# Expert feed-forward of a two-layer encoder: the first pair's rows are half gathered by products, half by an indirect DMA

## The chip, the cores and the metric

The kernel runs on one core of one Trainium2 chip. The metric is device time in microseconds (us) of one execution, as the median of several runs. A lower number is better.

## What is computed

The program is two layers of an encoder over 512 tokens of width 1024. Each layer is a mixer (three kinds of attention heads) and then a feed-forward part with 16 experts, of which each chooses its own 64 tokens:

```python
def expert_choice_ffn(h, w_router, w_gate, w_up, w_down):
    cap = CAPACITY_FACTOR * S // N_EXPERTS              # 64
    logits = einsum('bsd,de->bse', h, w_router)
    affinity = softmax(logits, axis=-1)
    gate, idx = top_k(swapaxes(affinity, 1, 2), cap)    # per expert: 64 tokens
    xe = vmap(lambda hb, ib: hb[ib])(h, idx)            # the chosen rows of h
    a = einsum('becd,edf->becf', xe, w_gate)            # 1024 x 1408 per expert
    u = einsum('becd,edf->becf', xe, w_up)              # 1024 x 1408
    y = einsum('becf,efd->becd', silu(a) * u, w_down)   # 1408 x 1024
    y = y * gate[..., None]
    return scatter-add of y to the rows idx of a zero (S, D)
```

Here h is the normalised residual stream. All is float32. The change touches how the line `xe = ...` is done for the first two experts of a layer.

## The kernel before, in words

**The experts' loop.** The 16 experts are taken in 8 pairs, and a pair has one tile of 128 rows: 64 rows of each of its experts. Loop `for p in range(8)` (L1213) does a pair. For each pair the gate weights, then the up weights, then the down weights are streamed from HBM, in 8 loads each (L1219 and L1253 call `load`, which issues the DMA at L153 from the queue of SP). One load is 128 partitions of 2 x 1408 floats, 1,441,792 bytes: one block of 128 input features for both experts. So a pair has 24 loads, and a layer 192.

**The ring of buffers.** Loads land in 15 buffers (`SEQ`, L35) that are taken in turn; one of them, `hx`, serves once, so from then on it is 14. A load can be issued only when the product that read the buffer's previous content is done. While the attention part still runs, SP has already issued the first 15 loads of the layer (gate 0 to 7 and up 0 to 6 of pair 0). Load 15 waits for the product with load 0, load 16 for the one with load 1, and so on to load 26; from load 27 on a load waits for the product 14 loads before it. Counted so, loads 8 to 15 are pair 0's up weights, 16 to 23 its down weights, and load 24 is the first gate load of pair 1.

**Products.** For feature block k of a pair the product is L1222: 12 instructions of TensorE, with `xe[:, k]` (features on partitions, the pair's 128 rows along the free axis) as stationary operand, and the weights moving. `keep_in_program_order` pins the products to the order in which the code is written; other instructions may be moved by the scheduler.

**How a pair's rows come into `xe`.** There are two ways.

- By products, for pair 0 alone. `places(0)` (L1123) makes a 0/1 selection matrix `at` from the router's ranks, scaled by the rows' normalisation factors. `fill(at, xe, k, n, pin)` (L1136) multiplies block k of the residual stream `x`, which is in SBUF, with it (L1142) and copies the result with a gain into `xe` (L1145, VectorE). The table `EARLY` (L57) says after which gate product which block is filled: block 0 ahead of the loop, blocks 1 and 2 after product 0, and one more block after each of the products 1 to 5.
- By an indirect DMA, for pairs 1 to 7. `marks(p)` (L1147) makes the selection matrix `oh` once more (VectorE), multiplies it with a small table (L1154) to get the token number and the scale of each row, transposes it for the later scatter (L1156), and copies the numbers to SBUF (L1158 to L1162). `fetch_rows(p)` (L1166) then has GpSimd start a DMA that reads 128 rows of 4 KB from the DRAM copy `xrow_d` of the residual stream (written before, L1025), and ScalarE scales them (L1170). `turn_rows` (L1173) transposes four 128x128 pieces of the rows (L1177) and copies them with the gain into `xe` (L1178). For pair p + 1 `marks` and `fetch_rows` stand after gate product 6 of pair p, and the two calls of `turn_rows` in the code after the up product of pair p (L1242). These transposes weren't pinned.

`marks(0)` (L1229) is needed for pair 0's scatter alone; it stands after up product 2 of pair 0.

**After the up product** of a pair silu(a) * u is formed (L1237 on ScalarE, L1238 on VectorE), transposed (L1246), copied (L1247) and multiplied with the down weights (L1259). The next pair's gate products carry the scatter of this pair's result (L1198).

Of the kernel before, what the change touches and what calls it, by code (L numbers as in the profile page):

```python
# [11 lines left out]
F32 = mybir.dt.float32  # L12
F32R = mybir.dt.float32r
# [9 lines left out]
P = 128  # L23
S = 512
D = 1024
L = 2
NT = S // P
# [26 lines left out]
PLAN = [(0, 1), (1, 1), (2, 2), (3, 2), (4, 2), (0, 0), (1, 2), (5, 2)]  # L54
PART_ON = 'vvav'
START = [[6, 0, 2, 6, 4], [2, 0, 0, 4, 2]]
EARLY = [[(0, 1)], [(1, 1), (2, 1)], [(3, 1)], [(4, 1)], [(5, 1)], [(6, 1)], [(7, 1)], [], []]  # L57
END_ON = 'avavav'
MARK_AT = 6
FIRST_MARKS = 2  # L60
SCATTER_AT = (2, 4)
HALVED = 8
EASE = 5
# [66 lines left out]
def body(ctx, tc, x_in, pos, w_in, w_uq, w_ukv, w_out, w_gate, w_up, w_down, gatt, gfin, params, consts, band, sel, out):  # L130
    nc = tc.nc
# [7 lines left out]
    def nm(s):  # L139
        uid[0] += 1  # L140
        return f"{s}_{uid[0]}"

    def bank():
        return pp.tile([P, 512], F32, tag="ps", name=nm("ps"))
# [17 lines left out]
    ident = cp.tile([P, P], F32, name="ident")  # L162
# [698 lines left out]
    for l in range(L):  # L861
        with ExitStack() as es:
# [186 lines left out]
            t = NT - 1  # L1049
# [16 lines left out]
            b = bank()  # L1066
# [4 lines left out]
            b = bank()  # L1071
# [11 lines left out]
        with tc.tile_pool(name=f"fx{l}", bufs=1, reuse_waits="tile") as fx, tc.tile_pool(name=f"fw{l}", bufs=2, side="right", reuse_waits="tile") as fw:  # L1083
# [24 lines left out]
            token, scales = slots[:, 128:136].bitcast(I32), slots[:, 136:144]  # L1108
# [13 lines left out]

            def places(p):  # L1123

                at_ = fw.tile([P, D], F32, tag="xy", bufs=1, name=nm("at"))[:, :S].rearrange("p (t s) -> p t s", t=NT)
                for t in (0, 2):
                    chosen(at_, p, t, t + 2)
                for t in range(NT):
                    if t < 2:
                        nc.scalar.activation(at_[:, t], at_[:, t], AF.Copy, scale=rstds[:, t : t + 1])  # L1130
                    elif t % 2 == 0:
                        q = at_[:, t : t + 2]
                        nc.vector.tensor_tensor(q, q, rstds[:, t : t + 2].unsqueeze(2).to_broadcast([P, 2, P]), op=ALU.mult)
                return at_

            def fill(at_, xe, k0, n, pin=False):  # L1136

                b = bank()
                for k in range(n):
                    c = (k0 + k) * P  # L1140
                    for t in range(NT):
                        made = nc.tensor.matmul(b[:, k * P : (k + 1) * P], x[:, t, c : c + P], at_[:, t], start=(t == 0), stop=(t == NT - 1))  # L1142
                        if pin:
                            tc.keep_in_program_order(made)
                nc.vector.tensor_tensor(xe[:, k0 : k0 + n, :], b[:, : n * P].rearrange("p (k s) -> p k s", k=n), gf[:, k0 : k0 + n].unsqueeze(2).to_broadcast([P, n, P]), op=ALU.mult)  # L1145

            def marks(p):  # L1147

                oh = fw.tile([P, S], F32R, tag="oh", bufs=2, name=nm("oh"))
                o3 = oh.rearrange("p (t s) -> p t s", t=NT)  # L1150
                tc.keep_in_program_order(chosen(o3, p, 0, NT))
                b, g = bank(), bank()
                for t in range(NT):
                    nc.tensor.matmul(g[:, 0:4], o3[:, t].bitcast(F32), info[:, t, p, :], start=(t == 0), stop=(t == NT - 1))  # L1154
                for t in range(NT):
                    nc.tensor.transpose(b[:, t * P : (t + 1) * P], o3[:, t].bitcast(F32), ident)  # L1156
                for i in range(2):
                    nc.vector.tensor_copy(gates[64 * i : 64 * i + 64, p : p + 1], g[64 * i : 64 * i + 64, i : i + 1])  # L1158
                if p > 0:
                    nc.vector.tensor_copy(token[:, p : p + 1], g[:, 2:3])  # L1160
                    nc.vector.tensor_copy(scales[:, p : p + 1], g[:, 3:4])
                nc.vector.tensor_copy(oh, b)  # L1162
                return oh


            def fetch_rows(p):  # L1166

                v = fw.tile([P, D], F32, tag="xy", bufs=1, name=nm("rows"))
                nc.gpsimd.indirect_dma_start(v, None, xrow_d[l][:, :], bass.IndirectOffsetOnAxis(token[:, p : p + 1], 0))  # L1169
                nc.scalar.activation(v, v, AF.Copy, scale=scales[:, p : p + 1])  # L1170
                return v

            def turn_rows(v, xe, k0):  # L1173

                b = bank()
                for k in range(4):
                    nc.tensor.transpose(b[:, k * P : (k + 1) * P], v[:, (k0 + k) * P : (k0 + k + 1) * P], ident)  # L1177
                nc.vector.tensor_tensor(xe[:, k0 : k0 + 4, :], b.rearrange("p (k s) -> p k s", k=4), gf[:, k0 : k0 + 4].unsqueeze(2).to_broadcast([P, 4, P]), op=ALU.mult)  # L1178

            def gathered():  # L1180
# [27 lines left out]
            xe, xg = gathered(), places(0)  # L1208
            warm(WARM_P)
            for f in EARLY[0]:  # L1210
                fill(xg, xe, *f)
            ohs = {}
            for p in range(8):  # L1213
                acc = []
                for w in (w_gate, w_up):
                    bs = [bank() for _ in cuts]
                    acc.append(bs)
                    for k in range(KD):
                        ws = load(w[l, p, k])  # L1219
                        for b, (q0, qn) in zip(bs, cuts):  # L1220
                            for i in range(2):
                                tc.keep_in_program_order(nc.tensor.matmul(b[64 * i : 64 * i + 64, : qn * NJ], xe[:, k, 64 * i : 64 * i + 64], ws[i][:, q0 * NJ : (q0 + qn) * NJ], start=(k == 0), stop=(k == KD - 1)))  # L1222
                        if w is w_gate and p == 0:
                            for f in EARLY[k + 1]:
                                fill(xg, xe, *f, pin=True)
                        if w is w_gate and k in SCATTER_AT and pending is not None:
                            scatter(*pending, 2 * SCATTER_AT.index(k))
                        if w is w_up and k == FIRST_MARKS and p == 0:
                            ohs[0] = marks(0)  # L1229
                        if w is w_gate and k == MARK_AT and p < 7:  # L1230
                            ohs[p + 1] = marks(p + 1)
                            rows = fetch_rows(p + 1)
                hx = wide()
                hh, hT = hx[:, :FF].rearrange("p (j q) -> p j q", j=NJ), hx[:, FF:].rearrange("p (j s) -> p j s", j=NJ)
                for g, u, (q0, qn) in zip(acc[0], acc[1], cuts):
                    hv = hh[:, :, q0 : q0 + qn].rearrange("p j q -> p q j")
                    nc.scalar.activation(hv, g[:, : qn * NJ].rearrange("p (q j) -> p q j", j=NJ), AF.Silu)  # L1237
                    nc.vector.tensor_tensor(hv, u[:, : qn * NJ].rearrange("p (q j) -> p q j", j=NJ), hv, op=ALU.mult)  # L1238
                if p < 7:
                    nxt = gathered()  # L1240
                    for k0 in (0, 4):
                        turn_rows(rows, nxt, k0)  # L1242
                for j0, n in ((0, 4), (4, 4), (8, 3)):
                    b = bank()
                    for q in range(n):
                        nc.tensor.transpose(b[:, q * P : (q + 1) * P], hh[:, j0 + q, :], ident)  # L1246
                    nc.vector.tensor_copy(hT[:, j0 : j0 + n, :], b[:, : n * P].rearrange("p (q s) -> p q s", q=n))  # L1247
                bs = [bank(), bank()]
                ahead = [(t, h) for t in range(NT - 1) for h in range(2)] if p == 7 else []
                whole = {}  # L1250
                for lo in range(0, NJ * D, FF):
                    hi = lo + FF
                    ws = load(w_down[l, p, lo // FF])  # L1253
                    e = lo
                    while e < hi:
                        j, h = e // D, e % D // 512
                        z = min(hi, (e // 512 + 1) * 512)
                        for i in range(2):
                            tc.keep_in_program_order(nc.tensor.matmul(bs[h][64 * i : 64 * i + 64, e % 512 : e % 512 + z - e], hT[:, j, 64 * i : 64 * i + 64], ws[i][:, e - lo : z - lo], start=(j == 0), stop=(j == NJ - 1)))  # L1259
                        e = z  # L1260
                    if ahead and lo > 0:
                        take_x(*ahead.pop(0))
                ys = results(p, bs)
                if p < 7:
                    pending = ohs.pop(p), ys
                    xe = nxt
            yh, yl = ys
            oh = ohs.pop(7)
# [17 lines left out]
            else:  # L1286
                rows = [slot(f"s{i}") for i in range(RING)]
# [112 lines left out]
```

## Time and the profile before

| | |
|---|---|
| median of 3 runs | 1974.07 us (1973.97 to 1975.56) |
| the profiled execution's own time | 1974.58 us |
| its span, first to last instruction | 1972.8 us |
| TensorE busy (PE) | 1754.5 us, 89% of the span |
| VectorE, ScalarE, GpSimd busy | 739.9, 425.0, 290.8 us |
| HBM read | 616.55 MB |
| L1222, gate and up products | 3072 instructions, some 570 to 590 ns each |
| L1142, products that gather (both layers) | 128 instructions |
| L1177, transposes of fetched rows | 112 instructions |

An instruction's line is that of kernel.py. PE is TensorE's matmuls, DVE VectorE, ACT ScalarE, POOL GpSimd; SP issues the weight loads. "ps" is a bank of PSUM, "xslot", "slot" and "hx" are the ring's buffers, "rows" the fetched rows. Times on the axis are from the span's start. Layer 0's expert loop runs from about 351 to 984 us, that of layer 1 from about 1320 us to the end.

### The profile page before, as it was taken

To read this page: it belongs to the slowest core of one execution; us is meant where nothing else is said; L and a number is where in the kernel's file an instruction comes from. 1 tells how busy PE (TensorE), PEld (TensorE's weight loads), DVE (VectorE), ACT (ScalarE), POOL (GpSimd) and SP (SyncE) were. 2 spreads that over 40 slices of the span, in tenths; PEclk is the share of its full clock that TensorE was granted. 3 is DMA by queue.
4 is the path that set the end of the run, shared out by engine and by line. 5 is a ranking of instruction groups with operands and counts; after the bars stand their busy time and mean duration, and the time that the engine had idled before them with its cause. 6 is when DMAs were issued, how large, how long until landed. Compare 5 with 4: busy or idle time off the path is not lost.

```text
span 1972.8 us, 22329 instructions
## 1 busy us (share of the span) xinstructions
PE 1754.5 (89%) x8894; PEld 918.0 (47%) x8894; DVE 739.9 (38%) x1467; ACT 425.0 (22%) x881; POOL 290.8 (15%) x276
## 2 busy tenths in 40 slices
PE   8889999898998988888898899998998988888887
PEld 6667666433333333333386756753333433333323
DVE  7886966111111111211178778551211211211112
ACT  4226972000000000000042379411000000000001
POOL 4552431000000000000055344200000000000000
PEclk9999999999999999999999999999999999999999
DMA  6755548899999999999947546488999999999995
GB/s 220 197 164 91 121 142 322 317 402 423 424 425 424 425 424 425 424 423 425 406 128 224 141 82 158 161 334 346 425 425 424 424 425 424 425 425 424 425 424 245
DMA packets 102473, 646.72 MB, mean 328 GB/s; under 512 B 11009, under 2 KB 28161, under 8 KB 53217
## 3 DMA queue, kind: packets, MB, share of 16 engines
q1 hardware_dynamic: 88336, 606.34, 76.7%
q0 software_dynamic: 11968, 35.02, 7.6%
q10 hardware_dynamic: 2064, 3.93, 0.6%
q8 instruction: 70, 1.15, 0.2%
q14 instruction: 35, 0.28, 0.0%
HBM read 616.55 MB, written 27.39 MB: 326 GB/s over the span
## 4 chain that ended last, share of the span: by engine, by line
DMA 39%; PE 37%; DVE 14%; issue 5%; ACT 3%; POOL 1%; SPq 0%; DVEq 0%; ACTq 0%; POOLq 0%
DMA xslot<-in_w_up_dram 13%; PE ps L1222 10%; DMA xslot<-in_w_gate_dram 10%; PE ps L1259 8%; DMA xslot<-in_w_down_dram 7%; PE ps L840 4%; DMA rows<-xrow_d,slots 3%; DMA slot<-in_w_gate_dram 3%; DMA slot<-in_w_down_dram 3%; PE ps L750 2%; PE ps L741 2%; PE ps L659 2%; PE ps L642 2%; DVE sm L591 1%; DVE sw L409 1%
## 5 line engine op out<-in xcount | busy, mean ns | idle before, releaser
L1222 PE MATMUL ps<-xslot,xe 128*64 128x506 f32 (+1 forms) x2400 | 515.8, 575 | 25.5 <-DMA xslot<-in_w_up_dram 13.3
L1222 PEld LDWEIGHTS ps<-xslot,xe 128*64 128x64 f32 x2400 | 167.0, 140 | 347.3 <-issue 288.5
L1259 PE MATMUL ps<-xslot,hx 128*64 128x512 f32 (+3 forms) x1392 | 248.6, 506 | 22.3 <-DMA xslot<-in_w_down_dram 18.4
L1238 DVE TENSOR_TENSOR hx<-ps,hx 128x506 f32<-128x506 f32 (+1 forms) x48 | 42.9, 957 | 473.9 <-PE ps L1222 473.9
L1259 PEld LDWEIGHTS ps<-xslot,hx 128*64 128x64 f32 x1392 | 94.2, 137 | 164.5 <-issue 123.4
L1189 ACT ACTIVATE hx<-ps,gates 128x512 fp32r<-128x512 f32 x32 | 20.2, 683 | 674.7 <-PE ps L1259 674.7
L1169 POOL DMA_INDIRECT rows<-xrow_d,slots x14 | 13.8, 984 | 985.2 <-DVE oh L1162 913.7
L1190 DVE SCALAR_TENSOR_TENSOR hx<-ps,gates,hx 128x512 fp32r<-128x512 f32 x32 | 22.6, 747 | 344.6 <-ACT hx L1189 344.6
L1222 PE MATMUL ps<-slot,xe 128*64 128x506 f32 (+1 forms) x648 | 141.8, 573 | 7.7 <-DMA slot<-in_w_gate_dram 6.0
L741 PE MATMUL ps<-xh,w 128*128 128x512 f32 (+1 forms) x448 | 142.6, 400 | 3.1 <-DVE w L340 2.4
L1200 DVE TENSOR_TENSOR x<-ps,x 128x512 f32<-128x512 f32 x112 | 69.6, 684 | 161.9 <-PE ps L1198 161.9
L598 ACT ACTIVATE P<-ps,sm 128x512 f32<-128x512 f32 x168 | 116.4, 703 | 41.1 <-DVE sm L591 40.0
L1170 ACT ACTIVATE rows<-rows,slots 128x1024 f32<-128x1024 f32 x14 | 16.1, 1147 | 446.0 <-DMA rows<-xrow_d,slots 446.0
L328 POOL TENSOR_TENSOR slot<-slot,gcol 128x1024 f32<-128x1024 f32 (+4 forms) x46 | 88.1, 1929 | 119.8 <-PE ps L1275 109.8
L741 PEld LDWEIGHTS ps<-xh,w 128*128 128x128 f32 (+1 forms) x448 | 83.3, 187 | 25.9 <-DVE w L340 3.3
L1222 PEld LDWEIGHTS ps<-slot,xe 128*64 128x64 f32 x648 | 45.3, 139 | 93.6 <-issue 75.8
L1177 PE MATMUL ps<-ident,rows 128*128 128x128 f32 x112 | 26.7, 417 | 66.5 <-ACT rows L1170 66.5
L741 PE MATMUL ps<-xl,w 128*128 128x512 f32 (+1 forms) x224 | 85.7, 393 | 0.0
L591 DVE TENSOR_REDUCE sm<-ps 128x1 f32<-128x512 f32 x120 | 78.9, 681 | 8.1 <-PE ps L576 5.7
L642 PE MATMUL ps<-ident,P 128*128 128x128 f32 x512 | 78.0, 275 | 0.3 <-ACT P L598 0.3
L1259 PE MATMUL ps<-slot,hx 128*64 128x512 f32 (+3 forms) x400 | 71.6, 497 | 6.2 <-DMA slot<-in_w_down_dram 4.7
L750 PE MATMUL ps<-w,xh 128*128 128x320 f32 (+1 forms) x256 | 65.9, 342 | 10.4 <-DVE w L340 10.4
(280 smaller groups left out, 2299.1 us busy)
## 6 DMA issues: line engine op xcount, KB each, us to landing
xslot<-in_w_gate_dram SPq DMA_DIRECT2D x100, 1408.0 KB, 26.2
xslot<-in_w_up_dram SPq DMA_DIRECT2D x100, 1408.0 KB, 27.1
xslot<-in_w_down_dram SPq DMA_DIRECT2D x100, 1408.0 KB, 27.0
slot<-in_w_gate_dram SPq DMA_DIRECT2D x28, 1408.0 KB, 27.0
slot<-in_w_down_dram SPq DMA_DIRECT2D x28, 1408.0 KB, 27.0
slot<-in_w_up_dram SPq DMA_DIRECT2D x26, 1408.0 KB, 27.4
slot<-in_w_in_dram SPq DMA_DIRECT2D x8, 1536.0 KB, 6.8
st<-bst_d POOLq DMA_DIRECT2D x40, 256.0 KB, 4.7
```

What stands on the lines that cost most here:

```text
L328: tc.keep_in_program_order(nc.gpsimd.tensor_tensor(v, v, g, op=ALU.mult))
L591: nc.vector.tensor_reduce(mn, ps, axis=AX.X, op=ALU.min)
L598: nc.scalar.activation(e, ps, AF.Exp, bias=mn, scale=-1.0, accum_out=lcol)
L642: nc.tensor.transpose(b[:, kc * P : (kc + 1) * P], e[:, kc * P : (kc + 1) * P], ident)
L659: nc.tensor.matmul(o[64 * i : 64 * i + 64], heads[2 * m + i][4][:, kc, :], pts[i][:, kc, :], start=(kc == 0), stop=(kc == NT - 1))
L741: nc.tensor.matmul(b[:m], w[:, passes[j][0], k, :m], passes[j][1](k), start=(n == 0), stop=(n == 3 * KD - 1))
L750: nc.tensor.matmul(acc[t][:, :m], xs, w[:, c, kk, :], start=(k == 0 and j == 0), stop=(k == KD - 1 and j == 2))
L840: nc.tensor.matmul(blocks[t][1 + h], o, w[h], start=(i == 0), stop=(i == 3 * KD - 1))
L1200: nc.vector.tensor_tensor(xv, b, xv, op=ALU.add)
L1222: tc.keep_in_program_order(nc.tensor.matmul(b[64 * i : 64 * i + 64, : qn * NJ], xe[:, k, 64 * i : 64 * i + 64], ws[i][:, q0 * NJ : (q0 + q ...
L1238: nc.vector.tensor_tensor(hv, u[:, : qn * NJ].rearrange("p (q j) -> p q j", j=NJ), hv, op=ALU.mult)
L1259: tc.keep_in_program_order(nc.tensor.matmul(bs[h][64 * i : 64 * i + 64, e % 512 : e % 512 + z - e], hT[:, j, 64 * i : 64 * i + 64], ws[i][ ...
```

## The change

Pair 0 now uses both ways. Blocks 0 to 3 of `xe` are still filled by products (`EARLY` is cut to them). Blocks 4 to 7 come by the indirect DMA: `marks(0)` moves to the place after gate product 0 (`FIRST_MARKS = 0`, now counted in the gate), followed by `fetch_rows(0)`, and `turn_rows(rows, xe, 4)` stands after gate product 3 (`HALF_AT = 3`). `marks` therefore writes token and scale for pair 0 too. `places` takes its tile from the two buffers tagged `oh` (512 wide) where it took the buffer of the fetched rows, which is now free for pair 0's rows. Last, the transposes in `turn_rows` are pinned to the written order, for every pair. Each layer has one more indirect DMA (8 where there were 7) and one more scaling on ScalarE.

The order below shows TensorE's queue at three places. First: layer 0, right after the product with block 0 (ps_3369 and ps_3375 are the banks of blocks 1 and 2, xslot_3330 and xslot_3333 the weights of gate loads 1 and 2). Before:

```order
L1142 MATMUL ps_3369<-at_3345,x 128x128 x4
L1142 MATMUL ps_3375<-at_3345,x 128x128 x4
L1222 MATMUL ps_3359<-xslot_3330,xe_3344 64x506 x2
L1222 MATMUL ps_3360<-xslot_3330,xe_3344 64x506 x2
L1222 MATMUL ps_3361<-xslot_3330,xe_3344 64x396 x2
L1142 MATMUL ps_3388<-at_3345,x 128x128 x4
L1222 MATMUL ps_3359<-xslot_3333,xe_3344 64x506 x2
```

The same place of the changed kernel (L1143, L1155 and L1157 are the old L1142, L1154 and L1156; oh_3381 is pair 0's selection matrix):

```order
L1143 MATMUL ps_3369<-at_3345,x 128x128 x4
L1143 MATMUL ps_3375<-at_3345,x 128x128 x4
L1155 MATMUL ps_3384<-slots_3340,oh_3381 128x4 x4
L1157 MATMUL ps_3383<-ident,oh_3381 128x128 x4
L1222 MATMUL ps_3359<-xslot_3330,xe_3344 64x506 x2
L1222 MATMUL ps_3360<-xslot_3330,xe_3344 64x506 x2
L1222 MATMUL ps_3361<-xslot_3330,xe_3344 64x396 x2
L1143 MATMUL ps_3408<-at_3345,x 128x128 x4
```

Pair 0's marks now stand ahead of gate product 1.

Second, TensorE's queue where fetched rows are first transposed. Before, this is in the up product of pair 0: xslot_3335 and xslot_3336 hold up loads 0 and 1, oh_3506 is pair 0's selection matrix, rows_3472 are pair 1's rows.

```order
L1222 MATMUL ps_3482<-xslot_3335,xe_3344 64x506 x2
L1222 MATMUL ps_3483<-xslot_3335,xe_3344 64x506 x2
L1222 MATMUL ps_3484<-xslot_3335,xe_3344 64x396 x2
L1154 MATMUL ps_3509<-slots_3340,oh_3506 128x4 x4
L1156 MATMUL ps_3508<-ident,oh_3506 128x128 x4
L1177 MATMUL ps_3567<-ident,rows_3472 128x128 x4
L1177 MATMUL ps_3573<-ident,rows_3472 128x128 x4
L1222 MATMUL ps_3482<-xslot_3336,xe_3344 64x506 x2
```

In the changed kernel it is between gate products 3 (slot_3421) and 4 (xslot_3331), and the rows are pair 0's (rows_3398); oh_3457 is pair 1's selection matrix.

```order
L1222 MATMUL ps_3359<-slot_3421,xe_3344 64x506 x2
L1222 MATMUL ps_3360<-slot_3421,xe_3344 64x506 x2
L1222 MATMUL ps_3361<-slot_3421,xe_3344 64x396 x2
L1177 MATMUL ps_3429<-ident,rows_3398 128x128 x4
L1222 MATMUL ps_3359<-xslot_3331,xe_3344 64x506 x2
L1222 MATMUL ps_3360<-xslot_3331,xe_3344 64x506 x2
L1222 MATMUL ps_3361<-xslot_3331,xe_3344 64x396 x2
L1155 MATMUL ps_3460<-slots_3340,oh_3457 128x4 x4
L1157 MATMUL ps_3459<-ident,oh_3457 128x128 x4
```

Four transposes stand there in place of eight, and between products 4 and 5 stand the marks of pair 1.

Third, TensorE's queue at the end of pair 0's up product, where xslot_3551 or xslot_3538 is the last up load and hx holds silu(a) * u. Before:

```order
L1222 MATMUL ps_3482<-xslot_3551,xe_3344 64x506 x2
L1222 MATMUL ps_3483<-xslot_3551,xe_3344 64x506 x2
L1222 MATMUL ps_3484<-xslot_3551,xe_3344 64x396 x2
L1246 MATMUL ps_3579<-ident,hx_3559 128x128 x4
L1246 MATMUL ps_3585<-ident,hx_3559 128x128 x4
L1246 MATMUL ps_3591<-ident,hx_3559 128x128 x3
```

The changed kernel (L1249 is the old L1246):

```order
L1222 MATMUL ps_3484<-xslot_3538,xe_3344 64x506 x2
L1222 MATMUL ps_3485<-xslot_3538,xe_3344 64x506 x2
L1222 MATMUL ps_3486<-xslot_3538,xe_3344 64x396 x2
L1177 MATMUL ps_3554<-ident,rows_3474 128x128 x4
L1177 MATMUL ps_3560<-ident,rows_3474 128x128 x4
L1249 MATMUL ps_3566<-ident,hx_3546 128x128 x4
L1249 MATMUL ps_3572<-ident,hx_3546 128x128 x4
L1249 MATMUL ps_3578<-ident,hx_3546 128x128 x3
```

The eight transposes of the next pair's rows now stand between the up product and the transposes of silu(a) * u. Pairs 1 to 6 and layer 1 have the same.

The diff:

```diff
 START = [[6, 0, 2, 6, 4], [2, 0, 0, 4, 2]]
-EARLY = [[(0, 1)], [(1, 1), (2, 1)], [(3, 1)], [(4, 1)], [(5, 1)], [(6, 1)], [(7, 1)], [], []]
+EARLY = [[(0, 1)], [(1, 1), (2, 1)], [(3, 1)], [], []]
+HALF_AT = 3
...
-FIRST_MARKS = 2
+FIRST_MARKS = 0
...
             def places(p):
 
-                at_ = fw.tile([P, D], F32, tag="xy", bufs=1, name=nm("at"))[:, :S].rearrange("p (t s) -> p t s", t=NT)
+                at_ = fw.tile([P, S], F32R, tag="oh", bufs=2, name=nm("at")).bitcast(F32).rearrange("p (t s) -> p t s", t=NT)
...
-                if p > 0:
-                    nc.vector.tensor_copy(token[:, p : p + 1], g[:, 2:3])
-                    nc.vector.tensor_copy(scales[:, p : p + 1], g[:, 3:4])
+                nc.vector.tensor_copy(token[:, p : p + 1], g[:, 2:3])
+                nc.vector.tensor_copy(scales[:, p : p + 1], g[:, 3:4])
                 nc.vector.tensor_copy(oh, b)
...
                 for k in range(4):
-                    nc.tensor.transpose(b[:, k * P : (k + 1) * P], v[:, (k0 + k) * P : (k0 + k + 1) * P], ident)
+                    tc.keep_in_program_order(nc.tensor.transpose(b[:, k * P : (k + 1) * P], v[:, (k0 + k) * P : (k0 + k + 1) * P], ident))
...
                         if w is w_gate and p == 0:
-                            for f in EARLY[k + 1]:
+                            for f in EARLY[k + 1] if k + 1 < len(EARLY) else ():
                                 fill(xg, xe, *f, pin=True)
+                            if k == FIRST_MARKS:
+                                ohs[0] = marks(0)
+                                rows = fetch_rows(0)
+                            if k == HALF_AT:
+                                turn_rows(rows, xe, 4)
                         if w is w_gate and k in SCATTER_AT and pending is not None:
                             scatter(*pending, 2 * SCATTER_AT.index(k))
-                        if w is w_up and k == FIRST_MARKS and p == 0:
-                            ohs[0] = marks(0)
                         if w is w_gate and k == MARK_AT and p < 7:
```

## Rows read from the trace of the kernel before

**Rows 1.** The page: what the DMA engines moved, in 40 slices.

```profile
GB/s 220 197 164 91 121 142 322 317 402 423 424 425 424 425 424 425 424 423 425 406 128 224 141 82 158 161 334 346 425 425 424 424 425 424 425 425 424 425 424 245
```

**Rows 2.** Stretches of layer 0: us, busy by engine, clock, DMA share, GB/s.

```profile
376.00:390.00 14.00, 8.32 (x52) 4.66 (x51) 2.76 (x9) 1.65 (x2) 1.23 (x1) 0.88 1.00 423
390.00:396.00 6.00, 6.00 (x26) 2.72 (x26) 0.00 (x0) 0.78 (x1) 0.00 (x0) 0.71 0.13 54
396.00:411.00 15.00, 13.68 (x72) 4.95 (x69) 3.22 (x5) 2.63 (x3) 0.00 (x0) 1.00 0.99 388
411.00:945.00 534.00, 470.26 (x2399) 188.75 (x2397) 90.67 (x159) 33.18 (x41) 6.23 (x7) 0.97 1.01 424
```

**Rows 3.** Stretches of layer 1, the same view.

```profile
1359.00:1365.40 6.40, 6.40 (x26) 3.06 (x28) 0.00 (x0) 1.12 (x1) 0.00 (x0) 0.70 0.16 65
1380.00:1945.00 565.00, 497.31 (x2522) 199.75 (x2524) 95.49 (x165) 33.16 (x41) 5.64 (x6) 0.97 1.01 424
```

**Rows 4.** Timeline: issues of weight loads by SP (start, length, queue, line).

```profile
353.55 0.33 SPq L153 DMA_DIRECT2D xslot<-in_w_up_dram  x1
395.05 5.05 SPq L153 DMA_DIRECT2D xslot<-in_w_gate_dram  x3
406.87 0.33 SPq L153 DMA_DIRECT2D slot<-in_w_gate_dram  x1
```

**Rows 5.** Timeline: the first gate products and fills of layer 0.

```profile
350.93 2.59 PE L1222 MATMUL ps<-xslot,xe 128*64 128x506 f32 x12 [0.38 <-DVE xe L1145]
355.42 2.58 PE L1222 MATMUL ps<-xslot,xe 128*64 128x506 f32 x12
355.53 0.29 DVE L1145 TENSOR_TENSOR xe<-ps,pgf 128x128 f32<-128x128 f32 x1 [0.60 <-PE ps L1142]
357.94 1.16 PE L1142 MATMUL ps<-at,x 128*128 128x128 f32 x8
359.03 2.58 PE L1222 MATMUL ps<-xslot,xe 128*64 128x506 f32 x12
```

**Rows 6.** Timeline: pair 1's marks, gather, scaling and transposes.

```profile
375.95 1.05 PE L1154 MATMUL ps<-slots,oh 128*128 128x4 f32 x8
377.43 4.95 PE L1222 MATMUL ps<-xslot,xe 128*64 128x506 f32 x24
378.56 1.23 POOL L1169 DMA_INDIRECT rows<-xrow_d,slots  x1 [35.68 <-issue]
388.33 1.15 ACT L1170 ACTIVATE rows<-rows,slots 128x1024 f32<-128x1024 f32 x1 [38.78 <-DMA rows<-xrow_d,slots]
389.54 1.97 PE L1177 MATMUL ps<-ident,rows 128*128 128x128 f32 x8 [5.68 <-ACT rows L1170]
391.44 8.30 PE L1222 MATMUL ps<-xslot,xe 128*64 128x506 f32 x36
```

**Rows 7.** All 14 gathers: waits of the transposes (page), landing (the tile's view).

```profile
L1177 PE MATMUL ps<-ident,rows 128*128 128x128 f32 x112 | 26.7, 417 | 66.5 <-ACT rows L1170 66.5
DMA to landing us min/median/max: 9.3/9.7/10.6
```

**Rows 8.** The selection matrix, four transposes at full clock, the copy into xe.

```profile
373.75 0.68 DVE L1116 TENSOR_TENSOR oh<-iota,code 128x512 fp32r<-128x512 f32 x1
326.37 0.66 PE L934 MATMUL ps<-ident,x 128*128 128x128 f32 x4
L1178 DVE TENSOR_TENSOR xe<-ps,pgf x28: 679/683/689, 410.4 to 1844.5; 128x512 f32<-128x512 f32 x28
```

**Rows 9.** The clock (column after POOL) at the transposes, view of stretches.

```profile
389.50:391.40 1.90, 1.86 (x8) 1.57 (x8) 0.00 (x0) 1.28 (x1) 0.00 (x0) 0.50 0.60 255
```

**Rows 10.** Timeline: the end of pair 0's up product.

```profile
406.66 2.53 PE L1222 MATMUL ps<-xslot,xe 128*64 128x506 f32 x12
410.51 1.42 PE L1246 MATMUL ps<-ident,hx 128*128 128x128 f32 x11 [1.32 <-DVE hx L1238]
```

**Rows 11.** Timeline: two products in the up part of pair 7.

```profile
942.78 2.58 PE L1222 MATMUL ps<-xslot,xe 128*64 128x506 f32 x12 [0.80 <-DMA xslot<-in_w_up_dram]
946.17 2.58 PE L1222 MATMUL ps<-xslot,xe 128*64 128x506 f32 x12 [0.80 <-DMA xslot<-in_w_up_dram]
```

## The prediction, made before the changed kernel was run

> **What bounds the kernel now.** I read the page's slices first. From about 400 us to the end of layer 0, and again in layer 1, the DMA engines move 423 to 425 GB/s in slice after slice [rows 1]. The stretches say the same more sharply: 424 GB/s from 411 to 945 us and from 1380 to 1945 us [rows 2, 3]. That is the weights' stream at its own speed. Late in a layer the products wait for it: in pair 7 each starts 3.39 us after the one before, of which it works 2.58 and waits 0.80 for its load [rows 11]. So from 411 us on nothing that TensorE saves can move the end, and only two things can: more or fewer bytes, and how long the stream stood still before. The place to look at is therefore the start of a layer's expert loop, and the question at each edit is when SP could issue the next load.
>
> There the order turns round. All 15 buffers are full when the first product starts at 350.93 [rows 5]. Load 15 goes out at 353.55, when product 0 has ended [rows 4], and the following ones at TensorE's pace: a product and a fill are 3.6 us from start to start (355.42 to 359.03), a little more than the 3.39 us a load takes. In the middle of pair 0's up part there is a hole. TensorE stands at the transposes of pair 1's rows for 5.68 us, until these have come and been scaled; the eight transposes take 1.97 us, the next three products 8.30 us in place of 3 x 2.48 [rows 6]. The clock is at 0.50 there, which is its 1.2 GHz level [rows 9]. So load 24, which waits for up product 1, goes out as late as 395.05 [rows 4]. Meanwhile the stream ran dry: 54 GB/s from 390 to 396, then 388 to 411 [rows 2]. Against 424 this is 6 x (1 - 54/424) = 5.2 us and 15 x (1 - 388/424) = 1.3 us of lost transfer time. Layer 1 has the same hole: 6.4 us at 65 GB/s are 5.4 us lost [rows 3].
>
> **The change, part by part.** All times are layer 0's.
>
> Marks of pair 0 behind gate product 0. The copy of block 2 starts at 355.53 and takes 0.29 [rows 5]; VectorE's comparison (0.68) [rows 8] stands behind it, so the selection matrix is ready at 356.5. TensorE, done with the fills at about 355.4, waits 1.1 us for it. The marks take it 1.48 us (375.95 to 377.43) [rows 6], so product 1 starts at 358.05 in place of 355.42, and load 16 follows at 360.7. The marks themselves are moved, not added: before they stood behind up product 0.
>
> The gather. From the marks' start to GpSimd's issue it was 378.56 - 375.95 = 2.61 us [rows 6], which gives 359.15. From issue to landing the 14 gathers took 9.3 to 10.6 [rows 7]; the first of a layer, seen at ScalarE, 9.77 (378.56 to 388.33) [rows 6]. I take 9.3: those gathers shared the DMA engines with a stream of 423 GB/s [rows 2], this one meets about one load at a time. That gives 368.45; with the scaling (1.15) [rows 6] the rows are ready at 369.6. A landing within 6.4 us would bring no wait, and at 10.6 it is 1.3 us later; both ends are kept.
>
> The Trainium skill, page "DMA: Bandwidth & Descriptors", section "Anatomy of one DMA — SWDGE (gpsimd) path", gives a DMA started by GpSimd about 2.0 us plus its bytes at 436 GB/s. For 524,288 bytes I estimate from it 3.2 us; the trace's 9.3 to 10.6 us speaks against it here [rows 7]. By the page the first rival below would hold.
>
> TensorE until then: product 1 (2.5), one fill (359.03 - 357.94 = 1.09) [rows 5], products 2 and 3 (2.5 each), done at 366.7. It waits 2.95 us, transposes four pieces (0.66 at full clock) [rows 8], and waits for VectorE's copy (0.68, rows 8, and about 0.1 of hand-over). Product 4 starts at 371.1, where before it started at 366.23 (two periods of 3.6 after 359.03), and would end at 373.7. The pause may pull the clock down as the 5.68 us did. That fall cost 1.97 - 2 x 0.66 = 0.65 for eight transposes and 8.30 - 7.44 = 0.86 behind; with four transposes at most 0.33 + 0.8 = 1.1 us. I take 0.6, between nothing and 1.1, since this pause is half as long. Load 19, which waits for product 4, thus goes out at 374.3.
>
> What follows has no holes. The fills of blocks 4 to 7 are gone, and so is the wait for pair 1's rows. Products 5 to 7 and up 0 and 1 take 2.48 us each, pair 1's marks 1.48: load 20 can go at 376.8, 21 at 379.3, 22 at 383.2, 23 at 385.7, 24 at 388.2. The stream wants them at steps of 3.39 from 374.3 on, so each buffer is free ahead of its turn.
>
> The sum. Load 24 has its turn at 374.3 + 5 x 3.39 + 1.24 (pair 1's gather, 524,288 bytes at 424 GB/s) = 392.5 in place of 395.05, a gain of 2.55 us. The second hole goes too: load 27 could go out only at 406.87 [rows 4], and now at about 398. Of the 1.3 us lost there I count 0.6, since a restart has some loss of its own and the changed kernel restarts too, at load 19. That is 3.15 us. The rest of the layer hangs on the stream, so its end moves by as much. The added gather (1.24 us of transfer) is inside: it falls before load 19, while TensorE paces the stream. Layer 1 has the same rows in all that I use, so two layers give 6.2 us.
>
> The pinned transposes. In pair 0 the last up product starts at 406.66 and TensorE stands for 1.32 us until 410.51 [rows 10]; eight transposes at full clock take 2 x 0.66 = 1.3 us and fit into that gap. Behind them are the transposes of silu(a) * u, which at 1.97 us would start 0.65 late, and the down product. That costs nothing while the stream is the bound. In the other pairs it takes away most of the 66.5 us that TensorE waited at L1177 [rows 7], and this I count at nothing too: the stream ran at 424 GB/s across those waits.
>
> The profiled execution took 1974.58 us, 1.8 more than its span and 0.5 above the median. The gain moves span and median alike: 1974.07 - 6.2 is about 1968.
>
> **The rivals.**
>
> 1. *The gather is quick.* Alone on the engines it lands within 6.4 us, there is no wait and no fall of the clock, and product 4 ends at about 370.8. For it: here the stream is not at full speed. Against it: no gather of the 14 took under 9.3 [rows 7]. The gain is limited by the transfers queued from 360.7 on (three loads and the gather, 11.4 us), so load 19 has its turn at 372.2: 5.2 us a layer, 1963.7; with a part of that, about 1965.
> 2. *The new wait gives most of it back.* Landing at 10.6 and the full 1.1 us of low clock bring load 19 to 376.1: 1.3 us a layer, 1971.4, which a measurement here can't tell from no change (that bound is about 0.2%, 4 us). For it: the pause is new and stands on TensorE alone.
> 3. *The gather is late, and the kernel slower.* Product 4 stands behind the rows in TensorE's queue, so each microsecond beyond 9.3 delays load 19 by one. With the clock as forecast the gain is gone at a landing of 9.3 + 3.15, about 12.5 us; at 14.5 it is a loss of 2 us a layer, 1978. For it: this is the first gather after the attention part, and GpSimd needed 1.23 us to start such a first one [rows 6]. Against it: that gather still landed in 9.77.
> 4. *The pins cost.* If the eight transposes delayed the stream in each of the 14 places by 1.3 us, this would be 18 us, less the gain: 1986. Against it: the loads for the down product are in their buffers by then.
>
> **How the numbers follow.** Forecast 0.63 (load 19 between 373.2 and 375.6, 1965.7 to 1970.5); rival 1 0.10, rival 2 0.19, rival 3 0.06, rival 4 0.02. The likeliest time is 1968.0. The range from 1964.5 to 1972.5 takes in rival 2 and the nearer part of rival 1 and leaves out rivals 3 and 4 and the end of rival 1. Faster by over 0.2% (under 1970.1): 0.57 of the forecast and rival 1, 0.67. Slower by over 0.2%: rivals 3 and 4 without their small part, 0.07. The same: 0.26.
>
> **What would show it.** After the change, right: gate product 4 of pair 0 begins 4 to 6 us later than before, with a wait of 2 to 4 us at the four transposes just ahead; SP issues load 19 near 374 and load 24 near 388 (in layer 0); no stretch near 54 GB/s between 390 and 396, and a shorter one near 370 to 375; hardly any wait left at L1177 in the other pairs, and 424 GB/s there as before. Wrong: load 19 after 377, a new hole later in pair 0, or a steady stretch below 424 GB/s.

## The result, and the profile after

| | before | after |
| --- | --- | --- |
| median of 5 runs, us | 1975.47 (1973.97 to 1976.05) | 1965.15 (1964.01 to 1965.51) |
| span of the profiled execution, us | 1972.8 | 1963.4 |
| mean granted clock of TensorE | 0.963 | 0.985 |

The ratio is 0.9946, with a 95% interval of 0.9935 to 0.9957: the change makes the kernel 10.3 us faster. The forecast was 6.2 us, and a time of 1968.0.

The page's slices of the changed kernel, as [rows 1]:

```profile
GB/s 221 196 164 93 122 127 323 338 425 423 424 424 425 423 425 425 425 424 425 407 133 224 141 88 159 144 333 400 424 424 424 424 425 424 424 425 424 425 424 248
```

The eighth slice (345 to 395 us before), in which layer 0's expert loop begins, went from 317 to 338 GB/s, the ninth from 402 to 425, and the 28th (1332 to 1381 us), in which layer 1's hole lay, from 346 to 400. The plateau behind them is what it was. The view of stretches is sharper (us, busy by engine, clock, DMA share, GB/s), first the four of [rows 2] with what stands ahead of them, then layer 1 as in [rows 3]; the two long stretches end 10 us earlier:

```profile
358.66:362.85 4.19, 4.19 (x14) 1.15 (x13) 0.80 (x3) 0.00 (x0) 1.09 (x1) 0.59 0.39 112
376.00:390.00 14.00, 14.00 (x74) 5.14 (x72) 0.00 (x0) 2.43 (x2) 0.18 (x1) 1.00 1.01 423
390.00:396.00 6.00, 6.00 (x34) 2.15 (x32) 0.00 (x0) 2.58 (x3) 0.00 (x0) 1.00 1.04 439
396.00:411.00 15.00, 14.29 (x89) 6.68 (x87) 5.58 (x8) 0.04 (x1) 0.00 (x0) 1.00 1.00 422
411.00:935.00 524.00, 452.60 (x2322) 174.67 (x2318) 88.61 (x154) 33.33 (x41) 6.20 (x7) 1.00 1.01 424
1359.00:1365.40 6.40, 6.06 (x37) 2.85 (x34) 3.38 (x5) 0.03 (x1) 0.00 (x0) 1.00 1.01 424
1380.00:1935.00 555.00, 478.29 (x2431) 183.97 (x2429) 93.16 (x160) 33.26 (x41) 5.61 (x6) 1.00 1.01 424
```

Both holes are gone: 54 GB/s became 439, and 65 became 424. The stretch behind the first hole rose from 388 to 422. No new hole stands later, and the steady rate is unchanged. One short dip is new, ahead of load 16: 112 GB/s from 358.66 to 362.85, where the kernel before had 269 from 358.02 to 362.20.

The timeline of pair 0, layer 0 up to 981 us and layer 1 behind it (start, length, engine, line; the number in brackets is the wait ahead and what ended it). Line numbers below L1160 are one higher than in [rows 4 to 6], those behind the product L1222 three higher, those between the same.

```profile
351.57 2.58 PE L1222 MATMUL ps<-xslot,xe 128*64 128x506 f32 x12 [0.38 <-DVE xe L1146]
...
357.21 1.03 PE L1155 MATMUL ps<-slots,oh 128*128 128x4 f32 x8 [1.07 <-DVE oh L1117]
358.66 4.25 PE L1222 MATMUL ps<-xslot,xe 128*64 128x506 f32 x12
359.71 1.09 POOL L1169 DMA_INDIRECT rows<-xrow_d,slots  x1 [15.94 <-DVE oh L1162]
362.96 3.93 SPq L154 DMA_DIRECT2D xslot<-in_w_down_dram  x2
364.26 1.15 ACT L1170 ACTIVATE rows<-rows,slots 128x1024 f32<-128x1024 f32 x1 [14.06 <-DMA rows<-xrow_d,slots]
...
368.81 0.66 PE L1177 MATMUL ps<-ident,rows 128*128 128x128 f32 x4
370.25 2.58 PE L1222 MATMUL ps<-xslot,xe 128*64 128x506 f32 x12 [0.78 <-DVE xe L1178]
372.88 4.32 SPq L154 DMA_DIRECT2D xslot<-in_w_down_dram  x2
...
386.32 9.78 SPq L154 DMA_DIRECT2D xslot<-in_w_gate_dram  x4
...
400.39 1.09 PE L1177 MATMUL ps<-ident,rows 128*128 128x128 f32 x8
401.83 1.42 PE L1249 MATMUL ps<-ident,hx 128*128 128x128 f32 x11 [0.35 <-DVE hx L1241]
...
980.72 3.95 PE L1278 MATMUL ps<-hx,oh 128*128 128x512 f32 x16 [0.79 <-ACT hx L1189]
...
1316.21 2.58 PE L1222 MATMUL ps<-xslot,xe 128*64 128x506 f32 x12 [0.38 <-DVE xe L1146]
...
1323.30 2.58 PE L1222 MATMUL ps<-xslot,xe 128*64 128x506 f32 x12
1324.30 1.07 POOL L1169 DMA_INDIRECT rows<-xrow_d,slots  x1 [16.24 <-PE ps L1157]
1325.92 3.93 SPq L154 DMA_DIRECT2D xslot<-in_w_down_dram  x2
1328.87 1.15 ACT L1170 ACTIVATE rows<-rows,slots 128x1024 f32<-128x1024 f32 x1 [14.03 <-DMA rows<-xrow_d,slots]
```

Four things are to be seen. The gather of pair 0 landed 4.55 us after its issue (359.71 to 364.26), and 4.57 us in layer 1. The four transposes at 368.81 have no bracket: TensorE did not wait for the rows, which were ready at 365.41. Product 1 took 4.25 us in layer 0 and 2.58 in layer 1; the granted clock was 0.59 over the first (0.50, its 1.2 GHz level, until 361.70) and 1.00, its 2.4 GHz level, over the second. And load 24 was issued at 386.32 where it was 395.05 [rows 4].

The rows' tile, all 16 gathers:

```profile
L1177 PE MATMUL ps<-ident,rows x120: 272/273/329, 368.8 to 1834.3; 128*128 128x128 f32 x120
DMA to landing us min/median/max: 4.5/9.4/10.6
```

The transposes run at 273 ns in the median, where it was 421 (the mean was 417 [rows 7]), and no wait for ScalarE is left of the 66.5 us. The two new gathers are the minimum. Seen at ScalarE, the other 14 took 8.4 to 10.7 us, where those before took 9.4 to 10.7.

The time is accounted for by two stretches. The kernel before ends layer 0 with the first of these rows of its timeline, and the second is layer 1's product 0:

```profile
984.47 3.94 PE L1275 MATMUL ps<-hx,oh 128*128 128x512 f32 x16 [0.79 <-ACT hx L1189]
...
1320.23 2.58 PE L1222 MATMUL ps<-xslot,xe 128*64 128x506 f32 x12 [0.38 <-DVE xe L1145]
```

From product 0 to this product it is 984.47 - 350.93 = 633.54 us before and 980.72 - 351.57 = 629.15 after: 4.39 less. From layer 1's product 0 to the end of the span it is 1972.8 - 1320.23 = 652.57 before and 1963.4 - 1316.21 = 647.19 after: 5.38 less. Together that is 9.8 us, and the span fell by 9.4: the first product of layer 0 comes 0.64 us later, and the attention part of layer 1 is 0.27 shorter, neither of which the change touches.

### The profile page after: what moved, and what is told of

Same layout as the page of the kernel before. It is cut to its first block, busy times and chain, and to the rows that moved or that the text cites. A ratio compares the mean times of both kernels' runs of the same rounds, so it can differ in the third digit from the quotient of the medians.

```text
span 1963.4 us, 22222 instructions
## 1 busy us (share of the span) xinstructions
PE 1734.6 (88%) x8838; PEld 892.7 (45%) x8838; DVE 739.6 (38%) x1465; ACT 427.8 (22%) x883; POOL 292.3 (15%) x278
## 4 chain that ended last, share of the span: by engine, by line
DMA 52%; PE 29%; DVE 13%; ACT 3%; issue 1%; POOL 1%; DVEq 0%; SPq 0%; ACTq 0%; POOLq 0%
DMA xslot<-in_w_up_dram 16%; DMA xslot<-in_w_gate_dram 14%; DMA xslot<-in_w_down_dram 14%; PE ps L1222 5%; PE ps L841 5%; PE ps L1262 4%; DMA slot<-in_w_up_dram 3%; DMA slot<-in_w_gate_dram 3%; DMA slot<-in_w_down_dram 3%; PE ps L751 2%; PE ps L742 2%; PE ps L660 2%; PE ps L643 2%; DVE sm L592 1%; DVE w L341 1%
## 5 line engine op out<-in xcount | busy, mean ns | idle before, releaser
L1222 PE MATMUL ps<-xslot,xe 128*64 128x506 f32 (+1 forms) x2400 | 508.2, 563 | 79.0 <-DMA xslot<-in_w_up_dram 57.9
L1222 PEld LDWEIGHTS ps<-xslot,xe 128*64 128x64 f32 x2400 | 160.8, 136 | 407.1 <-issue 257.5
L1222 PE MATMUL ps<-slot,xe 128*64 128x506 f32 (+1 forms) x648 | 140.3, 568 | 27.2 <-DMA slot<-in_w_up_dram 17.5
L1222 PEld LDWEIGHTS ps<-slot,xe 128*64 128x64 f32 x648 | 44.1, 137 | 117.7 <-issue 72.5
L751 PE MATMUL ps<-w,xh 128*128 128x320 f32 (+1 forms) x256 | 66.5, 344 | 10.4 <-DVE w L341 10.4
L651 ACT COPY pt<-ps 128x512 f32<-128x512 f32 x118 | 68.7, 603 | 26.4 <-PE ps L643 26.1
```

Source lines behind the costliest of these rows:

```text
L651: nc.scalar.copy(dv, bv)
L751: nc.tensor.matmul(acc[t][:, :m], xs, w[:, c, kk, :], start=(k == 0 and j == 0), stop=(k == KD - 1 and j == 2))
```

## The experiments

Theory A is that the hole at load 24 is all that the change takes away, so that either half of the change alone would do it. The rivals each credit another part of the edit, or the clock. A measure runs through all of them: how long after the start of layer 0's product 0 SP issued loads 16 and 19, and the length from that product to the one at 980.72 above (us). These are of the profiled execution, the median is of all. Experiments 1 to 4 ran on one chip, 5 to 8 on another; the kernel before took 1976.58 and 1976.41 there.

| kernel | load 16 out | load 19 out | length of layer 0 | median, us |
| --- | --- | --- | --- | --- |
| before | 7.1 | 17.9 | 633.54 | 1975.5 to 1976.6 |
| the change | 11.4 | 21.3 | 629.15 | 1965.15 |
| pins alone | 7.1 | 17.9 | 627.08 | 1961.68 |
| half gather, no pins | 9.7 | 19.6 | 628.18 | 1965.5 |
| early compare | 8.4 | 18.3 | 627.26 | 1961.56 |
| marks one product later | 7.1 | 23.8 | 631.44 | 1970.23 |
| the change again | 11.4 | 21.3 | 629.35 | 1964.96 |
| pins, marks in the up part | 7.1 | 17.9 | 626.97 | 1961.85 |
| early compare, marks in the up part | 8.4 | 18.3 | 627.21 | 1962.59 |

**1. Pins alone.** The kernel before, with the pin and nothing else:

```diff
-nc.tensor.transpose(b[:, k * P : (k + 1) * P], ...)
+tc.keep_in_program_order(nc.tensor.transpose(b[:, k * P : (k + 1) * P], ...))
```

> The kernel before with one edit: the transposes of fetched rows are pinned behind the up product. Pair 0 still gathers all 8 blocks by products. Theory A (the time came from the hole in the weights' stream at load 24, which the wait for pair 1's rows made): the wait at the transposes in pair 0's up part is gone, load 24 is issued near 386.5 us of the span in place of 395.05, the stream has no stretch near 54 GB/s at 390 to 396, and since loads 16 to 23 still go out every 3.6 us from 358 on, the stream is steady about 7 us earlier in each layer: near 1960 us, faster than the change itself. Rival B (it came from the four products that gather which pair 0 no longer does): no more than 1 to 2 us a layer are gained by the pins, 1971 to 1974. Rival C (the pins change nothing): 1975.

Measured: 1961.68 (1961.28 to 1962.34), ratio 0.9926 [0.9913, 0.994]. Its stretch and its timeline in layer 0:

```profile
390.00:396.00 6.00, 6.00 (x32) 2.14 (x30) 0.00 (x0) 3.32 (x4) 0.00 (x0) 1.00 1.01 428
```

```profile
379.39 1.23 POOL L1169 DMA_INDIRECT rows<-xrow_d,slots  x1 [35.68 <-issue]
...
387.24 9.78 SPq L153 DMA_DIRECT2D xslot<-in_w_gate_dram  x4
389.22 1.15 ACT L1170 ACTIVATE rows<-rows,slots 128x1024 f32<-128x1024 f32 x1 [38.83 <-DMA rows<-xrow_d,slots]
...
401.31 1.09 PE L1177 MATMUL ps<-ident,rows 128*128 128x128 f32 x8
```

The first gather of the layer takes as long as before (9.83 us), but TensorE no longer waits for it: the pins let the up products pass. The hole is gone at 428 GB/s. The pins alone give more than the whole change, so the gain does not need the half gather, and rivals B and C fall. What the pins give is what the hole had cost: layer 0 is 6.46 us shorter than before, and by [rows 2] the stream had lost 5.2 + 1.3 = 6.5 us there. Layer 1 is 7.0 shorter, against 5.4 [rows 3] and 1.4 (383 GB/s from 1365.40 to 1380).

**2. Half gather without pins.** The changed kernel with the diff above reversed.

> The changed kernel without the pins on the transposes of fetched rows, which then stand behind up product 0 again. Theory A: pair 1's gather is issued near 375 and its rows are scaled near 385, so TensorE waits about 1 us at these transposes in pair 0; load 24 goes out near 390, about when the stream wants it: 1964 to 1967, about as the changed kernel (1965). The waits come back in the other pairs and cost nothing. Rival D (the pins made the time, through the other pairs' waits): most of the gain is lost, 1971 to 1975.

Measured: 1965.5 (1963.54 to 1966.55), ratio 0.9945 [0.9931, 0.9958]. The stretch, the timeline, and the view of waits (sum, times, longest):

```profile
390.00:396.00 6.00, 6.00 (x34) 2.23 (x32) 0.00 (x0) 0.00 (x0) 0.00 (x0) 1.00 1.01 426
```

```profile
385.68 1.09 PE L1177 MATMUL ps<-ident,rows 128*128 128x128 f32 x8 [2.95 <-ACT rows L1170]
389.33 9.78 SPq L154 DMA_DIRECT2D xslot<-in_w_gate_dram  x4
```

```profile
PE ps L1177 <- ACT rows L1170: 58.5, 14, 5.5
```

The waits of the transposes are back, 58.5 us in sum, and the time is the same as with pins. Pair 1's gather is issued at 374.03 here, 4.5 us earlier than before [rows 6], so its wait is 2.95 us where it was 5.68, and load 24 goes out at 389.33, early enough. Either edit alone removes the hole. The pins on top of the half gather add nothing; the half gather on top of the pins costs some 3.5 us (1965.15 for 1961.68). In this kernel the low clock at product 1 came in layer 1 (4.12 us) and not in layer 0 (2.58), the reverse of the change, so each of the two has it once. The waits in the other pairs and the low clock behind them are worth nothing measurable, as the stream bounds there.

**3. Early compare.** VectorE's comparison for pair 0 is put ahead of the expert loop, so that the marks need not wait for it:

```diff
+first = compare(0)
 ohs = {}
...
-ohs[0] = marks(0)
+ohs[0] = marks(0, first)
```

> The changed kernel with pair 0's comparison (selection matrix, 0.68 us on VectorE) moved ahead of gate product 0, where VectorE has nothing to do. Theory A: the wait of 1.07 us ahead of pair 0's marks is gone, and in layer 0 the low clock behind it (product 1 took 4.25 us there, 2.58 in layer 1); load 16 goes out 1 to 3 us earlier, the gather shares the engines with it and takes 5 to 7 us in place of 4.6, still without a wait worth more than 1 us; load 19 goes out 1 to 3 us earlier: 1961 to 1964. Rival: the stream isn't held by load 16 to 19 there, 1965.

Measured: 1961.56 (1961.2 to 1963.84), ratio 0.9927 [0.9914, 0.9941].

```profile
356.18 0.95 PE L1159 MATMUL ps<-slots,oh 128*128 128x4 f32 x8
357.56 2.58 PE L1227 MATMUL ps<-xslot,xe 128*64 128x506 f32 x12
...
370.11 4.32 SPq L154 DMA_DIRECT2D xslot<-in_w_down_dram  x2
```

The wait of 1.07 us is gone, product 1 runs at full clock, and load 19 is issued 3.0 us earlier after product 0 than in the change (18.3 for 21.3). The kernel is 3.4 us faster than the change (1964.96 in experiment 5; ratios 0.9927 and 0.9943) for one wait of 1.07 us in each layer and, in layer 0, the low clock behind it. The gather took 5.12 us, as expected.

**4. Marks one product later.** `FIRST_MARKS = 1` in place of 0: marks and gather stand behind gate product 1, and the transposes where they were.

> The changed kernel with pair 0's marks and gather one product later (behind gate product 1 and the fill of block 3), the transposes still behind product 3. Theory A (the gather landed within 4.6 us because the DMA engines had nothing else to do): it is now issued while loads 16 and 17 move and takes 6 to 9 us; TensorE waits 2 to 6 us ahead of product 4, load 19 goes out later than in the changed kernel: 1966 to 1970. Rival E (the first gather of a pair is quick whatever else moves): 4.5 to 5 us, a wait of about 1 us, 1964 to 1966.

Measured: 1970.23 (1969.51 to 1975.55), ratio 0.9974 [0.9963, 0.9986].

```profile
370.19 0.66 PE L1177 MATMUL ps<-ident,rows 128*128 128x128 f32 x4 [2.38 <-ACT rows L1170]
371.63 4.28 PE L1222 MATMUL ps<-xslot,xe 128*64 128x506 f32 x12 [0.78 <-DVE xe L1178]
375.94 4.32 SPq L154 DMA_DIRECT2D xslot<-in_w_down_dram  x2
```

This is the prediction's picture made real: a wait of 2.38 us at the four transposes, product 4 in 4.28 us at a clock of 0.60, load 19 at 23.8. Layer 1 has the same (2.87 us, then product 4 in 4.96 at 0.50). About half of the gain goes, more in the profiled execution, which took 1972.35. The landing itself missed what was expected of it: 5.08 us (363.90 to 368.98).

**5. The change again,** beside experiments 6 to 8 on one chip.

> The changed kernel once more, on the chip of the three runs beside it: 1964 to 1966.

Measured: 1964.96 (1964.44 to 1966.31), ratio 0.9943 [0.993, 0.9957]. Product 1 of layer 0 took 4.28 us again.

**6. Pins, marks in the up part.** Experiment 1, with the next pair's marks moved from gate product 6 to up product 1, and pair 0's behind up product 3:

```diff
-MARK_AT = 6
-FIRST_MARKS = 2
+MARK_AT = 1
+FIRST_MARKS = 3
...
-if w is w_gate and k == MARK_AT and p < 7:
+if w is w_up and k == MARK_AT and p < 7:
```

> The pins alone, and the marks and gather of the next pair moved from behind gate product 6 to behind up product 1 (pair 0's own marks from up 2 to up 3), since the pinned transposes need the rows only at the end of the up product. Theory A (what counts is when the loads up to about 24 can be issued): the 1.48 us of marks no longer stand ahead of loads 22 and 23, the stream is steady 1 to 1.5 us earlier in each layer: 1958 to 1960. Rival: these marks are hidden by the stream already, 1961 to 1962 as with the pins alone.

Measured: 1961.85 (1960.58 to 1962.65), ratio 0.9925 [0.9912, 0.9939] against 1964.96 for the change on the same chip. Load 22 goes out at 379.51, 1.6 us earlier after product 0 than in experiment 1 (380.88), and the time does not move, as the rival said: from load 19 on the stream has what it can take.

**7. Extra traffic.** A copy of 4.2 MB out of the core's memory is started on ScalarE's queue as the first product begins, to see whether traffic lengthens the gather:

```diff
 xe, xg = gathered(), places(0)
+nc.scalar.dma_start(spare_d[l], xg.rearrange("p t s -> p (t s)").unsqueeze(1).to_broadcast([P, 16, S]))
```

> The changed kernel with a useless transfer of 4.2 MB from the selection matrix in SBUF to a spare DRAM buffer, begun on ScalarE's queue at about 350 us in each layer, so that the DMA engines are busy when pair 0's rows are gathered. Theory A (the gather is quick because the engines are idle): it takes 8 us or more in place of 4.6, TensorE waits ahead of product 4; with the added bytes (10 us a layer at 424 GB/s) 1980 to 1992. Rival E (the first gather is quick by itself): still 4.5 to 5 us and no wait there, with a time that only the added bytes raise.

Measured: one run, 2023.83, beside which the gather took 6.24 us:

```profile
361.04 1.09 POOL L1170 DMA_INDIRECT rows<-xrow_d,slots  x1 [15.93 <-PE ps L1158]
366.07 2.07 SPq L154 DMA_DIRECT2D xslot<-in_w_up_dram  x4
367.28 1.15 ACT L1171 ACTIVATE rows<-rows,slots 128x1024 f32<-128x1024 f32 x1 [15.75 <-DMA rows<-xrow_d,slots]
```

SP's own loads were late as well (none of pair 0's up loads went out before 366.07), and the whole time is over 30 us above what was expected, so neither the time nor the size of the effect can be read from it. The direction agrees with traffic, the size is below what was expected.

**8. Early compare, marks in the up part.** Experiment 3 with the moved marks of experiment 6 for pairs 1 to 7.

> The changed kernel with the comparison ahead of product 0, as in the earlier run that did that, and in addition the next pair's marks behind up product 1. Theory A: load 20 and later go out 1.5 us earlier, but from load 16 on the stream has little slack left: 1959.5 to 1961.5. Rival (the marks are the limit there): 1957 to 1959.

Measured: 1962.59 (1961.03 to 1964.05), ratio 0.9931 [0.9917, 0.9945]: no better than experiment 3, and 1 us above what was expected.

**9. A gather in the stream.** Experiment 1, with pair 0's marks and a gather of its rows, which nothing uses, behind gate product 4:

```diff
-FIRST_MARKS = 2
+FIRST_MARKS = 4
...
-if w is w_up and k == FIRST_MARKS and p == 0:
+if w is w_gate and k == FIRST_MARKS and p == 0:
     ohs[0] = marks(0)
+    fetch_rows(0)
```

> The pins alone (all 8 blocks of pair 0 by products), with pair 0's marks and gather placed behind gate product 4, where loads 18 to 20 are under way; its rows are used by nothing. One look, for the landing of a layer's first gather, of pair 0's rows. Theory A (its time goes by what else the DMA engines have to do): 7 to 10 us from issue to the scaling, against 4.55 in the changed kernel. Rival E (pair 0's gather is quick wherever it stands): 4.5 to 5 us. The time stays at 1961 to 1964, as nothing waits for these rows but the next pair's gather.

Measured: one run, 1966.93.

```profile
374.07 1.09 POOL L1168 DMA_INDIRECT rows<-xrow_d,slots  x1 [30.35 <-DVE oh L1161]
379.93 1.15 ACT L1169 ACTIVATE rows<-rows,slots 128x1024 f32<-128x1024 f32 x1 [29.78 <-DMA rows<-xrow_d,slots]
381.49 0.96 POOL L1168 DMA_INDIRECT rows<-xrow_d,slots  x1 [6.34 <-ACT rows L1169]
...
390.51 1.15 ACT L1169 ACTIVATE rows<-rows,slots 128x1024 f32<-128x1024 f32 x1 [9.44 <-DMA rows<-xrow_d,slots]
```

The first gather of the layer, now 14 us later than in the change, takes 5.86 us (6.15 in layer 1), and the next one, in the full stream, 9.02. It is between the two theories. That a gather is the layer's first does not make it quick: in experiment 1 the first one took 9.83. The time missed what was expected by 3 us: layer 0 is 628.95 long by the measure of the table, 1.9 more than in experiment 1, of which the added gather's transfer is 1.24. Load 20 also went out 2.6 us later after product 0 (24.1 for 21.5); whether that is the rest stays open.

## Why the prediction was right, and where its size was off

**Right: the place, and where the gain comes from.** The stream bounds, and the gain is the hole at load 24. The stretches of after show it closed, and experiments 1 and 2 each close it with one half of the edit.

**Right: the steps up to the gather.** On before's axis (0.64 us off for the later start) the wait for the comparison is 1.07 us (1.1 forecast), product 1 starts at 358.02 (358.05), GpSimd issues at 359.07 (359.15). The four transposes take 0.66, and product 4 then waits 0.78 for the copy, both as forecast.

**Mis-sized: "I take 9.3" for the gather.** It took 4.55 us. The 9.3 came from gathers in a stream of 423 GB/s [rows 2, 7], though the prediction itself said that this one would meet about one load at a time, and gave a bound of 6.4 us beside it. While this gather was under way the DMA engines moved 145 GB/s in layer 0 and 205 in layer 1. With it fell the wait of 2.95 us at the transposes and the low clock behind that pause; in this, rival 1 is what happened. The Trainium skill, page "DMA: Bandwidth & Descriptors", section "Anatomy of one DMA — SWDGE (gpsimd) path", from which I had estimated 3.2 us, was the nearer one here: 4.4 to 5.1 us where less else moved. For the 8.4 to 10.9 us in the full stream its fit does not hold.

**Misplaced: the clock.** I put a fall of 0.6 us behind the pause at product 4. In layer 0 it came at product 1, behind the wait of 1.07 us for the comparison: 4.25 in place of 2.58 us, 1.7 us. So load 16 went out at 362.32 on before's axis where I had 360.7. In layer 1, after the same wait, product 1 took 2.58, and load 16 was issued 9.71 us after product 0, at what would be 360.64.

**The sum.** Load 19 was forecast for 374.3 and went out at 372.24 on that axis, in layer 1 at what would be 370.57. With these the formula gives 3.15 + 2.1 = 5.2 and 3.15 + 3.7 = 6.9 us a layer; 4.39 and 5.38 were measured. So the formula, too, is a little steep: behind load 19 not each microsecond counts. By the table, against the shortest layer (627.0 with load 19 at 17.9), load 19 later by 1.7, 3.4 and 5.8 us made the layer 1.2, 2.2 and 4.4 us longer, some 0.6 to 0.8 for each (the last from experiment 4's profiled execution, 2 us above its median). Rival 1's cap of 5.2 us a layer was 0.2 short of layer 1.

**Partly luck: the hit.** The forecast proper ended at 1965.7. The measured 1965.15 is in the range because that took in a part of rival 1, which had a chance of 0.10. And two errors worked against each other: on one side the wait for the rows and the low clock at product 4, 2.95 and 0.6 us that never came, on the other the 1.7 us at product 1, which were not forecast. That load 19 went out at 372.24 in layer 0, where rival 1 has 372.2, is chance too: there the queued transfers set it, here the slow product 1; in layer 1 it is 370.57. Of the signs named beforehand, those of the hole came: load 24 at 385.7 on before's axis, no stretch near 54 GB/s, no wait at L1177. Those of the new pause did not: product 4 began 3.4 us later and not 4 to 6, nothing waited for the rows, and from 370 to 375 the stream ran at 401 GB/s.

**Two misreadings that moved nothing.** Load 27 went out at 404.50; the 406.87 of [rows 4] is load 28's, and the 0.6 us counted there came from the stretch, not from this time. Pair 1's marks stand between products 4 and 5, as the order under "The change" shows, and not ahead of product 7: load 20 went out 3.99 us after load 19 where 2.5 were counted. Experiment 8 took these marks away and gained nothing on experiment 3.

**Right: the pins cost nothing** (rival 4 falls). Eight transposes take 1.09 us at full clock, and L1249 behind them waits 0.35 where it waited 1.32 [rows 10]. What the prediction did not see is that they alone would do the whole work. It named TensorE's wait at the transposes of pair 1's rows as the cause of the hole, saw in the order that the pins take those transposes out from among the up products, and still counted the pins at nothing.

**A better version.** Pins alone (1961.68) and the change with the early compare (1961.56) are both 3 to 4 us below the change. Experiments 6 and 8 stay at the same level, 1961.9 and 1962.6: moving the later marks gave nothing more. Of the two, the pins are one line.

## What to carry to other kernels

Where a stream of loads bounds, look for the moment at which it ran dry, and ask which instruction stood in the queue ahead of the one that frees the buffer: pinning that instruction behind may cost nothing and be the whole gain. Try the parts of a change one at a time, as the larger part may only add a wait. A duration taken from a stretch of full traffic is not the duration in a quiet one; read first what else moves where the operation will stand.

## What the hardware showed

- A gather of 128 rows of 4 KB took 4.4 to 5.1 us from issue to landing where few loads were under way (5.6 in layer 1 of experiment 4), 5.9 to 6.4 beside a stream that TensorE paced or beside the 4.2 MB copy, and 8.4 to 10.9 in the full stream (11.5 once, in experiment 7). The busy share of the DMA engines between issue and landing rises in the same order: 0.47 to 0.80, 0.85 to 0.94, 0.97 to 1.03. One gather breaks it: pair 1's in layer 1 of experiment 4 took 5.1 us at a share of 1.01 (366 GB/s), issued 2.5 us after load 19 had restarted the stream. That traffic is the cause fits all but this one; no run changed the traffic alone, so it is not shown.
- After a wait of 1.07 us of TensorE ahead of pair 0's marks, the next product ran at a lower granted clock in layer 0 of the change, in both of its profiles (4.25 and 4.28 us in place of 2.58; 0.59 and 0.60), in layer 1 of experiment 2 (4.12) and in layer 1 of experiment 9 (4.28). Behind the same wait it took 2.58 in layer 1 of the change, in layer 0 of experiments 2 and 9, and in both layers of experiments 4 and 7. The eight transposes behind the 2.95 us in experiment 2 ran at full clock too (1.09 us). What decides it is not settled.
